# Feed-forward part of an encoder layer: the first product by one level of Strassen's scheme, its result through DRAM, the second product in two token halves

## The chip, the cores and the metric

The kernel runs on one core of a Trainium2 chip. The metric is device time in microseconds. The times of the kernel before are 1242.28, 1242.99 and 1244.46 us (median 1242.99). The traced execution spans 1241.3 us from its first to its last instruction. The engines are PE (matmuls, with PEld for its weight loads), DVE (vector), ACT (scalar), POOL and SP; SP issues the DMAs here.

## The reference

One DeepNorm encoder layer over 784 tokens: 16 meta tokens, 512 of a prompt and 256 of a sample (the last two give the 768 output rows). The model width is 1024, the feed-forward width 4096. The mixer (latent attention beside a bidirectional gated delta rule) is not touched; what follows it is

```
h  = layer_norm(alpha * h + mix, ln1_g, ln1_b)            # [768, 1024] real tokens
ff = square(relu(h @ w_ff1)) @ w_ff2                      # w_ff1 [1024, 4096], w_ff2 [4096, 1024]
h  = layer_norm(alpha * h + ff, ln2_g, ln2_b)             # alpha = 2 ** 0.25
return h[:, N_META:]
```

All of it is fp32. The kernel keeps that accuracy by splitting each operand of a matmul in a high and a low part (`split`: a cast on ACT, line 212, gives the high part, a subtraction on DVE, line 213, the low part) and adding three matmuls, high x high, high x low and low x high.

## The kernel before

The program has four stages: input norm and projections, delta rule, attention, and from about 640 us on the output projection, the first norm and the feed forward. Instructions are written in loops; a planner in the framework then sets each engine's order from its estimates of durations, and tiles of a pool go round in a fixed number of buffers, so that a new tile waits for the last reader of the one whose place it takes. Each engine works strictly in its order; SP issues the DMAs in its own order, and a DMA that waits holds back those behind it.

Tokens are taken in the order `TO` (six tiles of 128, two halves of 384). At the output projection, after three token tiles, `h1_half(0)` (L1065) transposes the normed tokens of one half on PE (L1069), scales them on ACT into `full` (L188) and splits them into `h1h`, `h1l`, features on partitions. After all six come the first matmuls of the feed forward on half 0 (`w1_mm`, L1058) for two weight tiles loaded ahead, then `h1_half(1)`.

The feed forward runs over 8 groups of `NG` = 4 tiles of 128 hidden features. For each tile `w1_load` (L1050) loads 128 columns of w_ff1 (0.52 MB) into the space `LTf` and splits them; `w1_mm` does 2 token halves x 8 feature tiles x 3 = 48 matmuls of 128x384 into a pair of PSUM banks `d` (L1061). ACT takes the relu out of PSUM (L1142), DVE squares (L1143), and the result is split into `fh`, `fl`. 128 rows of w_ff2 (0.52 MB) are loaded (L1150) and split into `w2h`, `w2l`. At the end of a group the second product runs: 6 token tiles x 2 column halves x 4 hidden tiles x 3 = 144 matmuls of 128x512 (L1167); each of the 12 PSUM banks of a group is added to `acc` in SBUF by DVE (L1171; the first group with the factor alpha, L1169). So PE does 1536 matmuls of 128x384 and 1152 of 128x512. The rows `rb2` scale `acc` for the residual (L1158). In the last group each token tile is normed, scaled (L1184 to L1186) and stored.

## Time and profile before

| what | value |
|---|---|
| median of three runs | 1242.99 us |
| profiled execution, span | 1241.3 us (1.7 below the median of the runs) |
| PE busy | 1168.4 us (94%), granted clock 0.973 on average |
| DVE busy | 717.2 us (58%) |
| ACT busy | 511.2 us (41%) |
| DMA moved | 126.49 MB, 102 GB/s on average |

A row of the profile names the line of the kernel, the engine, the operation, and the tiles written and read. Busy time is the sum over a group's instructions, a mean is of one, and matmuls overlap in the pipeline, so that the distance of two starts, not the mean duration of one, is what a matmul costs. The granted clock is a share of 2.4 GHz. A chain of waits follows the work that ended last back through what released each step.

### The profile page before, as it was taken

What the parts mean: (1) busy time and instruction counts of PE and PEld (TensorE: products, weight loads), DVE (VectorE), ACT (ScalarE), POOL (GpSimd) and SP (SyncE); (2) the same over time, 40 slices, a digit from 0 to 9 for tenths busy, and PEclk for the clock granted to TensorE, in tenths of its full rate; (3) what the DMA queues carried; (4) which work ended last, traced back from release to release, by engine and by line L of the source; (5) the groups of instructions that cost most, each with busy time, mean ns of one, the idle gap of its engine ahead of it and who ended that gap; (6) DMA issues with size and microseconds to landing.
All of it is one profiled execution on the core that took longest, in us unless ns stands there. A gap on an engine that the chain in (4) does not pass through costs nothing.

```text
span 1241.3 us, 18703 instructions
## 1 busy us (share of the span) xinstructions
PE 1168.4 (94%) x7468; PEld 1021.7 (82%) x7468; DVE 717.2 (58%) x1136; ACT 511.2 (41%) x974; POOL 171.8 (14%) x201
## 2 busy tenths in 40 slices
PE   5978879998999999989999899999999999999995
PEld 4867879998889877756758798989898989899994
DVE  8567668697967867684456584334243424343348
ACT  5475655324645666563545521203030303121113
POOL 2144554024223221020100000000000000000000
PEclk9888899999999999999999899999999999999998
DMA  5147764522497845340210230303030303131002
GB/s 202 50 111 182 183 166 142 122 92 90 143 268 220 250 132 137 124 140 31 93 52 35 85 102 30 106 24 114 1 119 17 119 18 102 35 100 36 1 1 102
DMA packets 92202, 126.49 MB, mean 102 GB/s; under 512 B 34946, under 2 KB 63362, under 8 KB 92114
## 3 DMA queue, kind: packets, MB, share of 16 engines
q1 hardware_dynamic: 92114, 125.28, 33.9%
q8 instruction: 59, 0.97, 0.3%
q14 instruction: 29, 0.24, 0.1%
HBM read 98.73 MB, written 26.53 MB: 101 GB/s over the span
## 4 chain that ended last, share of the span: by engine, by line
PE 78%; DVE 9%; DMA 5%; ACT 3%; issue 2%; SPq 1%; POOL 1%; DVEq 0%; ACTq 0%; POOLq 0%
PE d L1061 21%; PE b L1167 21%; PE d L331 7%; PE b L1103 5%; DMA x<-gD 3%; PE v L1000 3%; PE c L1003 3%; PE d L969 3%; PE d L704 2%; PE b L837 2%; PE b L853 2%; PE b L877 2%; PE b L870 2%; DVE LP L598 1%; DVE tm L596 1%
## 5 line engine op out<-in xcount | busy, mean ns | idle before, releaser
L1061 PE MATMUL d<-h1h,w1h 128*128 128x384 f32 x512 | 171.5, 337 | 1.3 <-ACT LT L1142 1.3
L1061 PE MATMUL d<-h1l,w1h 128*128 128x384 f32 x512 | 172.0, 336 | 0.0
L1061 PE MATMUL d<-h1h,w1l 128*128 128x384 f32 x512 | 171.9, 336 | 0.0
L1167 PE MATMUL b<-w2l,fh 128*128 128x512 f32 x384 | 151.3, 394 | 0.0
L1167 PE MATMUL b<-w2h,fh 128*128 128x512 f32 x384 | 150.5, 392 | 0.0
L1167 PE MATMUL b<-w2h,fl 128*128 128x512 f32 x384 | 147.6, 389 | 0.0
L1171 DVE TENSOR_TENSOR acc<-acc,b 128x512 f32<-128x512 f32 x84 | 55.9, 685 | 137.9 <-PE b L1167 137.9
L331 PE MATMUL d<-hTh,wl 128*128 128x384 f32 (+1 forms) x352 | 124.7, 354 | 4.2 <-DVE wl L213 4.2
L331 PE MATMUL d<-hTh,wh 128*128 128x384 f32 (+1 forms) x352 | 125.5, 356 | 2.1 <-ACT ks L188 2.1
L212 ACT CAST w2h<-LT 128x1024 fp32r<-128x1024 f32 x32 | 31.9, 1045 | 230.9 <-PE b L1167 212.3
L331 PE MATMUL d<-hTl,wh 128*128 128x384 f32 (+1 forms) x352 | 125.9, 358 | 0.1
L1061 PEld LDWEIGHTS d<-h1h,w1h 128*128 128x128 f32 x512 | 96.3, 189 | 2.7 <-ACT LT L1142 1.6
L1061 PEld LDWEIGHTS d<-h1l,w1h 128*128 128x128 f32 x512 | 96.7, 189 | 0.9 <-DVE h1l L213 0.3
L1061 PEld LDWEIGHTS d<-h1h,w1l 128*128 128x128 f32 x512 | 96.7, 189 | 0.6 <-DVE w1l L213 0.3
L213 DVE TENSOR_TENSOR w1l<-LT,w1h 128x1024 fp32r<-128x1024 f32 x32 | 39.2, 1224 | 88.9 <-ACT w1h L212 88.7
L1167 PEld LDWEIGHTS b<-w2h,fl 128*128 128x128 f32 x384 | 72.1, 188 | 16.1
L1167 PEld LDWEIGHTS b<-w2h,fh 128*128 128x128 f32 x384 | 72.1, 188 | 15.9
L1167 PEld LDWEIGHTS b<-w2l,fh 128*128 128x128 f32 x384 | 72.2, 188 | 13.7
L212 ACT CAST w1h<-LT 128x1024 fp32r<-128x1024 f32 x32 | 33.5, 1050 | 100.3 <-PE d L1061 100.2
L331 PEld LDWEIGHTS d<-hTh,wl 128*128 128x128 f32 x352 | 68.3, 194 | 6.7 <-DVE wl L213 4.6
L331 PEld LDWEIGHTS d<-hTh,wh 128*128 128x128 f32 x352 | 68.1, 193 | 6.7 <-issue 3.4
L331 PEld LDWEIGHTS d<-hTl,wh 128*128 128x128 f32 x352 | 68.1, 193 | 2.9 <-issue 1.5
(316 smaller groups left out, 2265.6 us busy)
## 6 DMA issues: line engine op xcount, KB each, us to landing
LT<-in_w_ff SPq DMA_DIRECT2D x64, 512.0 KB, 3.3
wr<-in_w_in SPq DMA_DIRECT2D x22, 512.0 KB, 3.3
x<-gD SPq DMA_DIRECT2D x16, 560.0 KB, 5.6
KV<-vD SPq DMA_DIRECT2D x26, 256.0 KB, 4.4
U<-UD SPq DMA_DIRECT2D x26, 256.0 KB, 5.2
UD<-ua SPq DMA_DIRECT2D x16, 256.0 KB, 5.1
wor<-in_w_out SPq DMA_DIRECT2D x8, 512.0 KB, 6.5
TB<-tD SPq DMA_DIRECT2D x52, 64.0 KB, 2.5
```

Source lines behind the costliest of these rows:

```text
L212: S.copy(hi, src)
L213: return (eng or V).tensor_sub(lo, src, hi.bitcast(F32))
L331: T.matmul(ps[:, s, :c1 - c0], lhsT=a[:, k, :], rhs=b[:, k, c0:c1], start=(k == 0 and i == 0), stop=(k == KT - 1 and i == 2))
L704: T.matmul(ps[:, s, :HR], lhsT=a[:, k], rhs=b[:, cs], start=(k == 0 and i == 0), stop=(k == 2 and i == 2))
L837: T.matmul(ps[:, j * P:(j + 1) * P], lhsT=TB[:, j], rhs=KV[:, j], start=True, stop=True)
L969: T.matmul(ps[:, :w], lhsT=q[:, qs], rhs=kt[:, k0:k0 + w], start=True, stop=True)
L1000: T.matmul(ps[:, t * P:(t + 1) * P], lhsT=p[:, c0:c0 + P], rhs=dg, start=True, stop=True)
L1003: T.matmul(po[:m, :nq], lhsT=Vs[j][:, t0 + bi, :m], rhs=pt[:, :nq], start=(bi == 0), stop=(bi == ntl - 1))
L1061: T.matmul(ps[:, s, :HR], lhsT=a[:, k, :], rhs=b[:, k, s * HR:(s + 1) * HR], start=(k == 0 and i == 0), stop=(k == KT - 1 and i == 2))
L1103: T.matmul(ps, lhsT=x[:, k, :], rhs=y[:, cs], start=(k == 0 and i == 0), stop=(k == 3 and i == 2))
L1167: T.matmul(ps, lhsT=a[:, qs], rhs=b[:, cs], start=(f == 0 and i == 0), stop=(f == NG - 1 and i == 2))
L1171: V.tensor_add(acc[:, ti, cs], acc[:, ti, cs], ps)
```

## The change

The first product is written as [C11 C12; C21 C22] = A B with A the transposed w_ff1 (its two halves of hidden features by its two halves of input features) and B the normed tokens (two halves of input features by the two token halves). Sixteen rounds `m` take the tiles m and m + 16 of hidden features together. Each has seven products of 12 matmuls 128x384 (L1073 in the changed kernel) on weight blocks or sums of them: with B11, T2, B21, T1, T3, B22 and T4, where the T's are differences of the token quadrants, made once (L1150 to L1163). In a round DVE makes four sums of weight blocks (s12 at L1174 and L1175, then L1186, L1191), ACT and DVE split seven weight operands, and DVE combines the seven PSUM results into four quadrants `fo_` in `LTf` (L1179 to L1195); one is copied by ACT (L1178). ACT does the relu and the square in SBUF (L1198, L1199), and the round's four quadrants (0.79 MB) are stored to the DRAM tile `FD` (L1200). PSUM is cut in two rings, `w` and `b`, of four banks each; weight operands have nine buffers.

The second product follows when all rounds are done, in two token halves. A half keeps its 3 token tiles x 2 column halves in six PSUM banks over all 32 hidden tiles, so `acc` is touched once per bank (12 times in all, L1264). For each half all of w_ff2 is loaded and split (`w2_load`, L1226) and the half's quadrants are read back from `FD` (`f_load`, L1218, 0.39 MB per round). The last `NL` = 4 hidden tiles are kept and run token tile by token tile, after which each is normed and stored as before. The places in `LTf`: rounds alternate between 0..1.5D and 1.5D..3D for `fo_` and between 3D..5D and 5D..7D for the weights; w_ff2 tile n lies in n % 4 * D.

```diff
...
+    fq = {}
+    HQ = 4
+    def w1_raw(m):
+        o = 3 * D + m % 2 * 2 * D
+        wr = LTf[:, o:o + 2 * D].rearrange("p (q k c) -> p q k c", q=4, k=HQ)
+        ld(wr[:, 0:2], I["w_ff1"][m].rearrange("p (q k) c -> p q k c", q=2))
+        ld(wr[:, 2:4], I["w_ff1"][m + 16].rearrange("p (q k) c -> p q k c", q=2))
+        return wr
+    def w1_split(src):
+        wh, wl = (fv.tile([P, HQ, P], F32R, name=n, bufs=9) for n in ("w1h", "w1l"))
+        split(src, wh, wl)
+        return wh, wl
+    def prod(w, n, ps=None):
+        ps = ps if ps is not None else nbank()
+        (wh, wl), (bh, bl) = w, fq[n]
+        for k in range(HQ):
+            for i, (a, b) in enumerate(((wh, bh), (wh, bl), (wl, bh))):
+                T.matmul(ps[:, :HR], lhsT=a[:, k, :], rhs=b[:, k, :],
+                         start=(k == 0 and i == 0), stop=(k == HQ - 1 and i == 2))
+        return ps[:, :HR]
+    nb = [0]
+    def nbank():
+        nb[0] += 1
+        return bank("bw"[nb[0] % 2])
+    RAW0 = 0
+    def h1_full(s, k, full):
+        ps = bank()
+        for i in range(3):
+            T.transpose(ps[:, i * P:(i + 1) * P], acc[:, s * 3 + i, k * P:(k + 1) * P], ident)
+        act(full, ps[:, :HR], AF.Identity, bias=col("l1b", k), scale=col("l1g", k))
+        return full
+    def raw0(k):
+        return LTf[:, RAW0 + k * HR:RAW0 + (k + 1) * HR]
     for half in range(2):
...
         if half == 1:
-            banks_set(b=4, d2=2)
+            banks_set(w=4, b=4)
...
-            h1h = h1p.tile([P, KT, NR], F32R, name="h1h")
-            h1l = h1p.tile([P, KT, NR], F32R, name="h1l")
+            eh = ExitStack()
+            h1p = pool(eh, "h1p", 1, "left")
+            for n in ("B11", "B21"):
+                fq[n] = [h1p.tile([P, HQ, HR], F32R, name=n + x) for x in "hl"]
...
-            ahead = {ft: w1_load(ft) for ft in range(2)}
+            ahead = {}
+            for m in range(2):
+                wr = LTf[:, 6 * D:7 * D].rearrange("p (q k c) -> p q k c", q=2, k=HQ)
+                ld(wr, I["w_ff1"][m].rearrange("p (q k) c -> p q k c", q=2))
+                ahead[m] = [w1_split(wr[:, i]) for i in range(2)]
...
                 if ti == 3:
...
+                    for k in range(KT):
+                        f = h1_full(0, k, raw0(k))
+                        split(f, *(x[:, k % HQ] for x in fq["B11" if k < HQ else "B21"]))
                 if ti == 5:
                     for w in ahead.values():
-                        w1_mm(*w, 0)
-                    h1_half(1)
+                        w[:] = [prod(x, n, bank("w")) for x, n in zip(w, ("B11", "B21"))]
     ex.close()
-    banks_set(b=4, d2=2)
...
+    eq = ExitStack()
+    hq = pool(eq, "hq", 1)
+    for n in ("T2", "T1", "T3", "B22", "T4"):
+        fq[n] = [hq.tile([P, HQ, HR], F32R, name=n + x) for x in "hl"]
+    fu = pool(eq, "fu", 2)
+    for k in range(HQ):
+        b12, b22 = (h1_full(1, k + HQ * i, fu.tile([P, HR], F32, name=n)) for i, n in enumerate(("p5s", "b22")))
+        split(b22, *(x[:, k] for x in fq["B22"]))
+        t1, t2 = (fu.tile([P, HR], F32, name=n) for n in ("u2", "u3"))
+        V.tensor_sub(t1, b12, raw0(k))
+        V.tensor_sub(b12, b22, b12)
+        V.tensor_sub(t2, b22, t1)
+        split(t2, *(x[:, k] for x in fq["T2"]))
+        split(t1, *(x[:, k] for x in fq["T1"]))
+        split(b12, *(x[:, k] for x in fq["T3"]))
+        V.tensor_sub(t2, t2, raw0(k + HQ))
+        split(t2, *(x[:, k] for x in fq["T4"]))
+    FD = dp.tile([16, P, 4, HR], F32, name="FD")
+    for m in range(16):
+        wr = w1_raw(m)
+        p1, p2 = ahead.get(m, (None, None))
+        if p1 is None:
+            p1 = prod(w1_split(wr[:, 0]), "B11")
+        o = m % 2 * 4 * HR
+        fo_ = LTf[:, o:o + 4 * HR].rearrange("p (q c) -> p q c", q=4)
+        sm1 = fv.tile([P, 2, HQ, P], F32, name="s12", bufs=2)
+        V.tensor_add(sm1[:, 0], wr[:, 2], wr[:, 3])
+        V.tensor_sub(sm1[:, 1], sm1[:, 0], wr[:, 0])
+        p6 = prod(w1_split(sm1[:, 1]), "T2")
+        u2 = fu.tile([P, HR], F32, name="u2")
+        S.copy(fo_[:, 0], p1)
+        V.tensor_add(u2, fo_[:, 0], p6)
+        if p2 is None:
+            p2 = prod(w1_split(wr[:, 1]), "B21")
+        V.tensor_add(fo_[:, 0], fo_[:, 0], p2)
+        p5 = prod(w1_split(sm1[:, 0]), "T1")
+        u4 = fu.tile([P, HR], F32, name="p5s")
+        V.tensor_add(u4, u2, p5)
+        V.tensor_sub(wr[:, 2], wr[:, 0], wr[:, 2])
+        p7 = prod(w1_split(wr[:, 2]), "T3")
+        u3 = fu.tile([P, HR], F32, name="u3")
+        V.tensor_add(u3, u2, p7)
+        V.tensor_add(fo_[:, 3], u3, p5)
+        V.tensor_sub(wr[:, 1], wr[:, 1], sm1[:, 1])
+        p3 = prod(w1_split(wr[:, 1]), "B22")
+        V.tensor_add(fo_[:, 1], u4, p3)
+        p4 = prod(w1_split(wr[:, 3]), "T4")
+        V.tensor_sub(fo_[:, 2], u3, p4)
+        for q in ((0, 1), (1, 4)):
+            f = fo_[:, q[0]:q[1]]
+            S.activation(f, f, AF.Relu)
+            S.activation(f, f, AF.Square)
+        st(FD[m], fo_)
+    eq.close()
+    ef.close()
+    eh.close()
+    e7 = ExitStack()
+    fw = pool(e7, "fw", 2)
+    fo = pool(e7, "fo", 1)
...
-    NG = 4
...
-            V.tensor_mul(rl, rl, rl)
...
-                    V.tensor_add(acc[:, ti, cs], acc[:, ti, cs], ps)
...
+    def f_load(s, m):
+        fr = fw.tile([P, 2, HR], F32, name="fr", bufs=2)
+        ld(fr, FD[m, :, s::2, :])
+        fh, fl = (fw.tile([P, 2, HR], F32R, name=n, bufs=3) for n in ("fh", "fl"))
+        split(fr, fh, fl)
+        return fh, fl
+    def w2_load(n, ft):
+        o = n % 4 * D
+        wr = LTf[:, o:o + D]
+        ld(wr, I["w_ff2"][ft * P:(ft + 1) * P, :])
+        wh, wl = (fw.tile([P, D], F32R, name=n, bufs=5) for n in ("w2h", "w2l"))
+        return split(wr, wh, wl), wh, wl
+    NL = 4
+    rb2 = None
+    seq = [(m, i) for m in range(16) for i in range(2)]
+    for s in range(2):
+        po = [[bank(x) for _ in range(2)] for x in (("w", "w", "b"), ("b", "w", "w"))[s]]
+        last = []
+        for n, (m, i) in enumerate(seq):
+            if i == 0:
+                fh, fl = f_load(s, m)
+            x, wh, wl = w2_load(n, m + 16 * i)
+            if s == 0 and n == 2:
+                rb2 = rows2(2)
+                for ti in range(6):
+                    for j, fn in enumerate((V.tensor_mul, V.tensor_add)):
+                        y = fn(acc[:, ti], acc[:, ti], rb2[:, j])
+                        tc.add_manual_dep(y.ins, x.ins.name, NOSYNC, reason="not before it is needed")
+                rb2 = rows2(4)
+            last.append((n, i, fh, fl, wh, wl))
+            if n >= len(seq) - NL and n < len(seq) - 1:
+                continue
+            for g in range(3):
+                for n_, i_, fh_, fl_, wh_, wl_ in last:
+                    qs = slice(g * P, g * P + P)
+                    for h in range(2):
+                        cs = slice(h * 512, h * 512 + 512)
+                        for j, (a, b) in enumerate(((fh_, wh_), (fh_, wl_), (fl_, wh_))):
+                            T.matmul(po[g][h], lhsT=a[:, i_, qs], rhs=b[:, cs], start=(n_ == 0 and j == 0),
+                                     stop=(n_ == len(seq) - 1 and j == 2))
+                if n == len(seq) - 1:
+                    ti = s * 3 + g
+                    t = TO[ti]
+                    a = acc[:, ti]
+                    for h in range(2):
+                        cs = slice(h * 512, h * 512 + 512)
+                        V.scalar_tensor_tensor(a[:, cs], a[:, cs], ALPHA, po[g][h], ALU.mult, ALU.add)
+                    mv = fw.tile([P, 2], F32, name="mv")
+                    dst = O["yp"][t * P:(t + 1) * P, :] if t < 4 else O["ys"][(t - 4) * P:(t - 3) * P, :]
+                    norm_stats(a, P, mv, fw)
+                    for h in range(2):
+                        cs = slice(h * 512, h * 512 + 512)
...
+                        st(dst[:, cs], a[:, cs])
+            last = []
+    e7.close()
...
```

SP's order in the feed forward before (names: `LT` is the space `LTf`; `rb2` the rows of the second norm), from the first groups on:

```order
L1053 DMA LT_525<-in_w_ff1 128x1024 x3
L1128 DMA rb2_7310<-in_rows 128x1024 x2
L1053 DMA LT_525<-in_w_ff1 128x1024
L1150 DMA LT_525<-in_w_ff2 128x1024 x3
L1053 DMA LT_525<-in_w_ff1 128x1024
L1150 DMA LT_525<-in_w_ff2 128x1024
L1053 DMA LT_525<-in_w_ff1 128x1024 x3
L1150 DMA LT_525<-in_w_ff2 128x1024 x4
L1053 DMA LT_525<-in_w_ff1 128x1024 x4
```

And in the changed kernel where the first product ends and the second begins (`FD` written at L1200, read back into `fr` at L1218):

```order
L1200 DMA FD_7014<-LT_525 128x1536 x2
L1226 DMA LT_525<-in_w_ff2 128x1024
L1218 DMA fr_9235<-FD_7014 128x2x384
L1218 DMA fr_9287<-FD_7014 128x2x384
L1213 DMA rb2_9298<-in_rows 128x1024 x2
L1200 DMA FD_7014<-LT_525 128x1536
L1226 DMA LT_525<-in_w_ff2 128x1024
L1218 DMA fr_9357<-FD_7014 128x2x384
L1218 DMA fr_9409<-FD_7014 128x2x384
L1226 DMA LT_525<-in_w_ff2 128x1024 x2
L1218 DMA fr_9461<-FD_7014 128x2x384
L1226 DMA LT_525<-in_w_ff2 128x1024 x5
```

Stores and loads that go through `FD` now stand among the loads of w_ff2, and the last of the stores stands behind two of `fr` and two of `rb2`.

ACT's order in the feed forward before, one stretch of a group with its relu (L1142) and its casts:

```order
L1142 ACTIVATE LT_525<-d2_9914 128x768
L212 CAST fh_9965<-LT_525 128x768
L212 CAST w1h_10105<-LT_525 128x1024
L1142 ACTIVATE LT_525<-d2_9979 128x768
L212 CAST fh_10030<-LT_525 128x768
```

And in the changed kernel at the same boundary, from the last round's relu (L1198) on:

```order
L1198 ACTIVATE LT_525<-LT_525 128x1152
L212 CAST w2h_9242<-LT_525 128x1024
L1199 ACTIVATE LT_525<-LT_525 128x1152
L212 CAST fh_9237<-fr_9235 128x768
L212 CAST fh_9289<-fr_9287 128x768
L212 CAST fh_9359<-fr_9357 128x768
L212 CAST w2h_9265<-LT_525 128x1024
```

The first casts of the second product are now interleaved with the last relu and square.

DVE's order before, where one group's sums to `acc` end and the next tiles' splits stand:

```order
L213 TENSOR_TENSOR w2l_8324<-LT_525,w2h_8323 128x1024
L1171 TENSOR_TENSOR acc_5093<-acc_5093,b_8183 128x512
L213 TENSOR_TENSOR w2l_8389<-LT_525,w2h_8388 128x1024
L213 TENSOR_TENSOR w2l_8454<-LT_525,w2h_8453 128x1024
L213 TENSOR_TENSOR w2l_8687<-LT_525,w2h_8686 128x1024
L213 TENSOR_TENSOR w1l_8329<-LT_525,w1h_8328 128x1024
L1143 TENSOR_TENSOR LT_525<-LT_525 128x768
L213 TENSOR_TENSOR fl_8254<-LT_525,fh_8253 128x768
L213 TENSOR_TENSOR w1l_8394<-LT_525,w1h_8393 128x1024
L1143 TENSOR_TENSOR LT_525<-LT_525 128x768
L213 TENSOR_TENSOR fl_8319<-LT_525,fh_8318 128x768
```

And in the changed kernel in the middle of the first product, from the last split that reads one round's weights (`w1l_8771`) past the sum `s12_8954`, which reads the weights loaded into the same place:

```order
L213 TENSOR_TENSOR w1l_8771<-LT_525,w1h_8770 128x512
L1190 TENSOR_TENSOR LT_525<-u3_8606,w_8573 128x384
L1193 TENSOR_TENSOR LT_525<-p5s_8586,w_8614 128x384
L213 TENSOR_TENSOR w1l_8796<-LT_525,w1h_8795 128x512
L1174 TENSOR_TENSOR s12_8954<-LT_525 128x512
L1195 TENSOR_TENSOR LT_525<-u3_8606,b_8632 128x384
L213 TENSOR_TENSOR w1l_8816<-s12_8812,w1h_8815 128x512
L1175 TENSOR_TENSOR s12_8954<-s12_8954,LT_525 128x512
L1186 TENSOR_TENSOR LT_525<-LT_525 128x512
L213 TENSOR_TENSOR w1l_8836<-LT_525,w1h_8835 128x512
L1191 TENSOR_TENSOR LT_525<-LT_525,s12_8812 128x512
L1179 TENSOR_TENSOR u2_8690<-LT_525,b_8677 128x384
```

The sums to `acc` are gone; in their place stand sums of weights and of PSUM results between the splits, and the sum of newly loaded weights stands four instructions behind the split that frees their place.

## Rows read from the trace of the kernel before

**Rows 1.** Span and mean granted TensorE clock of the core.

```profile
core 0: 1241.3 us, clock 0.973
```

**Rows 2.** The page's chain of waits: shares by engine, then by line.

```profile
PE 78%; DVE 9%; DMA 5%; ACT 3%; issue 2%; SPq 1%; POOL 1%; DVEq 0%; ACTq 0%; POOLq 0%
PE d L1061 21%; PE b L1167 21%; PE d L331 7%; PE b L1103 5%; DMA x<-gD 3%; PE v L1000 3%; PE c L1003 3%; PE d L969 3%; PE d L704 2%; PE b L837 2%; PE b L853 2%; PE b L877 2%; PE b L870 2%; DVE LP L598 1%; DVE tm L596 1%
```

**Rows 3.** Windows: stretch, length, busy us by engine, PEclk, DMA share, rate.

```profile
694.14:731.15 37.01, 31.38 (x170) 30.08 (x169) 26.35 (x33) 18.19 (x28) 0.00 (x0) 0.91 0.30 100
...
694.00:698.00 4.00, 1.18 (x10) 0.91 (x8) 2.68 (x7) 1.63 (x2) 0.00 (x0) 1.00 0.88 288
...
770.95:1195.41 424.46, 424.46 (x2170) 388.74 (x2170) 159.79 (x180) 93.92 (x105) 0.00 (x0) 1.00 0.18 60
...
1222.90:1241.30 18.40, 5.48 (x24) 4.15 (x23) 14.85 (x35) 5.80 (x11) 0.00 (x0) 0.72 0.31 114
```

**Rows 4.** Chain of waits within the feed forward: start us, us, what.

```profile
1071.37 2.76 PE b L1167 x12
...
1076.93 21.98 PE b L1167 x96
...
1098.91 30.18 PE d L1061 x174
...
1137.69 2.76 PE b L1167 x12
```

**Rows 5.** Timeline of PE, start of feed forward: start us, us, what, [idle].

```profile
698.61 1.09 PE L1069 MATMUL b<-cst,acc 128*128 128x128 f32 x4 [3.43 <-ACT acc L1111]
...
700.57 1.54 PE L1069 MATMUL b<-cst,acc 128*128 128x128 f32 x6 [0.88 <-ACT full L188]
...
702.87 0.52 PE L1061 MATMUL d<-h1h,w1l 128*128 128x384 f32 x1
...
703.19 0.52 PE L1061 MATMUL d<-h1h,w1h 128*128 128x384 f32 x1
...
714.04 0.45 PE L1061 MATMUL d<-h1h,w1h 128*128 128x384 f32 x1 [1.32 <-ACT LT L1142]
```

**Rows 6.** Groups from 640 us on: what, count, busy us, mean ns, idle.

```profile
L1171 DVE TENSOR_TENSOR acc<-acc,b 128x512 f32<-128x512 f32 x84 | 55.9, 685 | 137.9 <-PE b L1167 137.9
...
L212 ACT CAST w2h<-LT 128x1024 fp32r<-128x1024 f32 x32 | 31.9, 1045 | 230.9 <-PE b L1167 212.3 <-DMA LT<-in_w_ff 18.2 <-PE b L1103 0.4
...
L212 ACT CAST fh<-LT 128x768 fp32r<-128x768 f32 x32 | 26.7, 836 | 43.6 <-DVE LT L1143 43.6
...
L1158 DVE TENSOR_TENSOR acc<-acc,rb 128x1024 f32<-128x1024 f32 x12 | 13.9, 1217 | 0.0
...
L188 ACT ACTIVATE full<-b,cols 128x384 f32<-128x384 f32 x16 | 9.9, 666 | 1.5 <-DVE h1l L213 0.8 <-PE b L1069 0.7
...
L213 DVE TENSOR_TENSOR h1l<-full,h1h 128x384 fp32r<-128x384 f32 x16 | 8.3, 555 | 7.7 <-ACT h1h L212 7.7
...
L212 ACT CAST h1h<-full 128x384 fp32r<-128x384 f32 x16 | 7.4, 510 | 0.0
...
L1033 DVE TENSOR_TENSOR LT<-LT,v 128x384 f32<-128x384 f32 x8 | 4.2, 550 | 5.1 <-PE v L1032 4.8
...
L213 DVE TENSOR_TENSOR ml<-LT,mh 128x512 fp32r<-128x512 f32 x6 | 4.0, 683 | 1.0 <-ACT mh L212 1.0
...
L212 ACT CAST mh<-LT 128x512 fp32r<-128x512 f32 x6 | 3.6, 614 | 12.9 <-PE b L1103 7.7 <-DVE LT L1033 5.2
```

**Rows 7.** DMA issues: what, queue, count, KB each, median us to landing.

```profile
LT<-in_w_ff SPq DMA_DIRECT2D x64, 512.0 KB, 3.3
...
rb<-in_rows SPq DMA_DIRECT2D x6, 512.0 KB, 5.4
...
tD<-LT SPq DMA_DIRECT2D x6, 512.0 KB, 3.5
```

More of the change, by code (lines that the diff above doesn't have):

```diff
@@ L1064, in h1_half @@
-    def h1_half(s):
-        for k in range(KT):
-            ps = bank()
-            for i in range(3):
-                T.transpose(ps[:, i * P:(i + 1) * P], acc[:, s * 3 + i, k * P:(k + 1) * P], ident)
-            full = os_.tile([P, HR], F32, name="full")
-            cs = slice(s * HR, (s + 1) * HR)
-            act(full, ps[:, :HR], AF.Identity, bias=col("l1b", k), scale=col("l1g", k))
-            split(full, h1h[:, k, cs], h1l[:, k, cs])
+    fq = {}
[6 more added lines that the diff above has]
+        return wr
@@ L1122, in body @@
-    fw = pool(ef, "fw", 2)
-    fs = pool(ef, "fs", 2)
-    fo = pool(ef, "fo", 1)
+    eq = ExitStack()
[15 more added lines that the diff above has]
+        split(t2, *(x[:, k] for x in fq["T4"]))
@@ L1186, in body @@
                         V.tensor_add(a[:, cs], a[:, cs], rb2[:, 1, cs])
-                    st(dst[:, cs], a[:, cs])
-    ef.close()
+                        st(dst[:, cs], a[:, cs])
+            last = []
+    e7.close()
 def kernel(**inputs):
```

65 lines of the change are left out of this document (removed).

## Prediction

> **What bounds the kernel now.** I read the clock and span first [rows 1]: 0.973 of 2.4 GHz, so PE works at its upper level nearly throughout. The chain of waits comes next [rows 2]: PE holds 78% of it, and the two products of the feed forward 21% each; no other line comes near. The windows then show whether PE is the limit there at every moment [rows 3]: from 770.95 to 1195.41 us PE is busy in 424.46 of 424.46 us at clock 1.00, DVE in 160, ACT in 94, DMA has a share of 0.18. So a matmul taken out there is worth its full time, and anything on another engine is worth nothing until PE waits for it. The chain inside a group gives the prices [rows 4]: 174 matmuls of 128x384 in 30.18 us, 0.1734 each; 96 of 128x512 in 21.98 us, 0.229 each. They add up: a group from 1071.37 to 1137.69 is 66.32 us, and 192 x 0.1734 + 144 x 0.229 = 66.3. What the change adds therefore decides at three places: where the first product starts, whether its rounds keep PE fed, and where the second product begins.
>
> All sums go against the profiled span of 1241.3 us; the median of the runs lies 1.7 above it, which I add at the end.
>
> **Matmuls saved: -33.3.** 16 rounds x 7 x 12 = 1344 matmuls of 128x384 instead of 1536: 192 x 0.1734 = 33.3 us. The second product keeps its 1152.
>
> **Start of the first product: +4 (bounds +1 to +9).** Before, PE waits 0.88 and 1.32 us here, beside 3.43 for the normed tokens, which stays [rows 5]. After those waits matmuls start 0.32 apart (702.87, 703.19), the lower clock level, for about a dozen: 12 x (0.32 - 0.173) = 1.8. So 0.88 + 1.32 + 1.8 = 4.0 us were lost already. In the changed kernel 120 matmuls of the first two rounds (168 less the 48 done ahead), 20.8 us of PE, stand against the making of the second half's operands: per quadrant column 4 differences and 5 low parts, 36 DVE operations of 128x384 at 0.555 (the h1l row) behind one `full` of 0.67 [rows 6], so the last is ready 20.7 us after the first transpose. By the order 28 matmuls (4.9 us) stand behind it: 25.6 - 20.8 = 4.8. Two matmul groups (T4 of round 0, B11 of round 2) want PSUM banks which DVE frees late in this queue: +1.6, three operations of 0.55. Nine more weight splits and sums stand on DVE ahead of the norm of the last token tile, three of them not hidden: 3 x 0.68 = 2.0. Less the 4.0: 4.4, taken as 4. If DVE's backlog hides wholly behind the matmuls, only the bank waits remain (+1); if the cold stretch comes back and twice as many splits are exposed, +9.
>
> **The rounds: 0 (bounds 0 to +20).** PE needs 84 x 0.1734 = 14.56 us a round. DVE does 18 operations: 11 of 128x512 from SBUF at 0.683 (ml) and 7 of 128x384 from PSUM at 0.550 (L1033) [rows 6]: 11.4 us. To this comes one wait: the weights of a round go where those of the round before last lay, the split of its T4 operand frees the place, and the sum s12 of the new weights stands four instructions behind it on DVE. The three between cover 2 x 0.55 + 0.68 = 1.8 of it. A load of 0.52 MB takes 3.3 us where moving it at the 288 GB/s seen at most takes 1.8, so 1.5 goes otherwise [rows 3, 7]; with the round's other half (1.05 MB together) beside it, 3.6 + 1.5 = 5.1. The wait is 1.5 to 3.3; with its middle DVE is at 11.4 + 2.4 = 13.8, below PE's 14.56, with its end at 14.7, where the weight buffers' lead still covers 14 rounds. ACT is at 7 x 0.614 for casts, 0.51 for the copy, 2 x 0.51 and 2 x some 1.2 for relu and square (768 elements take 0.836, 1024 take 1.045, so 1152 some 1.2) = 8.2. The square on ACT has no row; between 0.84 and 2 us for the large one ACT stays under 11. The evictions that go (84 x 0.685 and 12 alike on DVE) lie beside PE: nothing gained. Upper bound: DVE 1.5 us above PE in 14 rounds.
>
> **From the first product to the second: +16 (bounds +10 to +20).** Count from the end of the last T4 matmul. DVE's last combination takes 0.6; the read of `fr` waits for it, since `fr` lies in the place of a round's buffer, and lands 3.3 to 4 later. ACT has in its order relu (1.2), cast of w_ff2 (1.05), square (1.2), cast of `fr` (0.84): the first matmul comes at 5. It finds one weight tile: 18 matmuls, 4.1 us, to 9.1. The next weight tile goes into a place that the last `FD` store still reads. That store waits for the square (4.2) and stands on SP behind two reads of `fr` (0.79 MB) and two loads of `rb2` (1.05 MB): these need 6.4 at 288 GB/s, to 7.0, its own 0.79 MB 2.7 more. With the 1.5 that goes otherwise, the store has landed at 11.3. Meanwhile w_ff2 tile 4 and two more reads of `fr` (1.31 MB) were issued ahead; they move until 14.4. Then the awaited tile, 1.8 + 1.5, to 17.7, and its cast, 1.05: the second group of matmuls starts at 18.7 instead of 4.1. That is 14.6 of loss, and 1.8 for the lower clock after such idling, as at the start: 16.4, taken as 16. Lower bound: every transfer in its own time by its nearest row, the store 1.5 x 3.5 from 4.2 to 9.4 [rows 7], the load 3.3 and the cast 1.05 to 13.8, less 4.1, 9.7. Upper bound: store and load each held up as the `rb` loads are (5.4 against 3.3), 2 x 2.1 more, 20.
>
> The Trainium skill speaks to this place ("DMA: Bandwidth & Descriptors", section "Anatomy of one DMA — SWDGE (gpsimd) path"): a transfer costs about 2.0 us fixed plus its bytes at 436 GB/s. By that estimate the store takes 3.8 and the load 3.2 (the row has 3.3), the group starts at 12.3 and the loss is 8.2. The rows show no rate above 288 GB/s, with 3.3 for one load alone and 5.4 for loads side by side; the page's fit is for another path than SP's queue.
>
> **The second product: 0.** A weight tile gives PE 18 x 0.229 = 4.1 us. Per two tiles (8.24 us) DMA brings 1.05 MB of w_ff2 and 0.39 MB of `fr`, 175 GB/s against the 288 seen; DVE has 2 x 1.22 (as L1158) + 0.95, ACT 2 x 1.045 + 0.836. Twelve operations of L1158's kind (14 us) are spread over slack. The second half starts in fresh banks with its loads ahead.
>
> **The end: -1 (bounds -2 to +1).** Before, the last window has PE busy for 5.48 of 18.40 us [rows 3], so matmuls end near 1228.4 and 12.9 us of eviction, norm and stores follow for two token tiles that DVE does together. After, the earlier tile is done under the 24 matmuls of the last: about 12.
>
> Sum: -33.3 + 4 + 0 + 16 + 0 - 1 = -14.3, a span of 1227.0; with the 1.7 of the median 1228.7, predicted as 1229. Own range 1219 to 1238, from the bounds of start and boundary.
>
> **Rivals.**
>
> *The boundary is cheap.* The reads, `rb2` and the store move side by side without holding each other up: its loss is 9.7 as in the lower bound, 6 less: 1223. For it: the DMA share is 0.18 in the feed forward, so nothing else is moving. Against it: at 694 to 698 the share is 0.88 at 288 GB/s, and the bytes ahead of the awaited tile are 4.5 MB. The Trainium skill's rule above would give 1221.
>
> *DVE becomes the bound of the rounds.* Place: the wait of s12 on its load. If the two weight loads move behind the `FD` store of a round (1.84 MB for all, 6.4 + 1.5 = 7.9 us), the wait is 6.1 and a round takes 17.5: 14 x 2.94 = 41, less what the nine weight buffers hold ahead, about four products x 2.08 = 8: +33, so 1262, slower than before. It decides from DVE rounds of 15.1 on (over 8 us in 14 rounds), and the kernel is slower than before from 16.2 (14 x 1.6 - 8 = 14.4), a wait of 4.8. For it: at most 0.8 us of slack in a sum of 18 prices. Against it: successive DVE operations overlap a little, and the store is issued half a round away from the loads.
>
> *The second product is short of data.* If the loads of w_ff2 and `fr` followed each other (3.9 + 2 x 3.3 = 10.5 us per two tiles against 8.24): 32 x 2.3 = 72, 1301. Against it: window rows with 0.88 DMA share show transfers running side by side, and 175 GB/s is well below that.
>
> *The matmuls saved come back as waits.* Start +9, boundary +20 and a few us in the rounds: about 1243, no change.
>
> **Chances.** Forecast 0.60, cheap boundary 0.13, DVE-bound rounds 0.14 (0.05 of it short of break-even, between 1231 and 1248), no change 0.07, short of data 0.05, something unforeseen 0.01. A measurement of this kernel can tell about 0.2% (2.5 us) from no change. Faster is the forecast, the cheap boundary and a part of the milder DVE case: 0.75; within 0.2% 0.07; slower 0.18 (the rest of the DVE case, the shortage, and the forecast with all its bounds on the bad side). The range goes from 1216 (the cheap boundary with a start at its lower bound, 1220, and a little for prices that overlap) to 1248 (the middle of the DVE case); outside lie the shortage, the full DVE case and a better end still, some 0.17.
>
> **What would show it.** Matmuls of the first product 1344 at starts 0.173 apart, and rounds of 14.6 us with PE busy throughout: right; DVE busy near 100% with PE idle "behind w1l" or a sum: the DVE case. At the boundary two gaps of PE, about 5 and 9.6 us, the second ended by a load of w_ff2: right; a second gap of 5 or less: the cheap boundary. In the second product PE gaps ended by DMA: the shortage. At the start a loss against before of 1 to 9 us on waits for DVE. Wrong altogether if the gaps sum to more than 33 us.

## The result, and the profile after

The changed kernel takes 1224.36 us (median of 4 runs, 1223.05 to 1226.39) against 1242.63 for the kernel before: ratio 0.9857, 95% interval 0.9839 to 0.9875, 18 us faster. 1229 was predicted, in a range of 1216 to 1248. The profiled execution spans 20.0 us less than that of before [rows 1]:

```profile
core 0: 1221.3 us, clock 0.973
```

The windows of the new profile (columns as in [rows 3]) show the stages one after the other: the start of the feed forward, the rounds, the boundary between the products, the second product, the end:

```profile
690.47:731.00 40.53, 32.96 (x179) 30.88 (x179) 36.87 (x80) 29.85 (x56) 0.00 (x0) 0.92 0.17 55
770.95:920.00 149.05, 149.05 (x859) 149.05 (x858) 103.83 (x178) 77.84 (x121) 0.00 (x0) 1.00 0.33 117
929.00:975.00 46.00, 33.34 (x128) 26.64 (x127) 30.65 (x29) 18.26 (x19) 0.00 (x0) 0.85 0.64 208
975.00:1060.00 85.00, 85.00 (x376) 70.39 (x376) 36.86 (x33) 29.56 (x31) 0.00 (x0) 1.00 0.62 209
1060.00:1195.00 135.00, 135.00 (x597) 111.78 (x597) 70.09 (x87) 51.02 (x60) 0.00 (x0) 1.00 0.50 166
1203.00:1221.30 18.30, 5.44 (x24) 4.16 (x23) 12.88 (x30) 3.81 (x8) 0.00 (x0) 0.77 0.23 86
```

In the rounds and in the second product PE is busy in every microsecond at clock 1.00, as it was [rows 3]. DVE has 104 of 149 us in the rounds. The two places where PE loses time are the first and the third window.

The prices of a matmul are read from the chain of waits (start, length, what, count), as in [rows 4]:

```profile
737.83 2.08 PE w L1073 x12
...
767.03 2.08 PE w L1073 x12
...
975.88 2.72 PE w L1256 x12
```

From 737.83 to 767.03 two rounds of 84 matmuls pass: 29.20 / 168 = 0.1738 each, so a round is 14.6 us. In the second product 12 take 2.72, that is 0.2267 each; before it was 0.2290 [rows 4]. That difference, times 1152, is 2.6 us.

The start of the feed forward on PE (idle before in brackets), answering to [rows 5]:

```profile
666.25 1.81 PE L1089 MATMUL b<-cst,acc 128*128 128x128 f32 x12
...
695.34 5.19 PE L1089 MATMUL b<-cst,acc 128*128 128x128 f32 x20 [4.27 <-ACT acc L1137]
...
701.82 0.45 PE L1073 MATMUL w<-T2h,w1h 128*128 128x384 f32 x1 [1.29 <-ACT T2h L212]
...
716.72 0.45 PE L1073 MATMUL w<-T4h,w1h 128*128 128x384 f32 x1 [1.34 <-DVE u L1179]
```

PE waits 4.27 for the normed tokens, 1.29 for the first operand and 1.34 for a PSUM bank (a further wait of 0.54 for an operand is not shown): 7.4 us where before it was 3.43 + 0.88 + 1.32 = 5.6. That the last of them is for a bank is read from DVE's row, which ends where the matmul starts and which reads a product of T2 out of PSUM; the first parts of T4 had been cast long before:

```profile
716.12 0.54 DVE L1179 TENSOR_TENSOR u<-LT,w 128x384 f32<-128x384 f32 x1
```

The first of PE's rows also says where this stage begins. In the kernel before the same transposes stand here:

```profile
670.57 1.82 PE L1069 MATMUL b<-cst,acc 128*128 128x128 f32 x12
```

They begin 4.3 us earlier now, ahead of everything that the prediction priced.

The boundary on PE: the last matmul of the first product, the first of the second, and the first on the second weight tile:

```profile
929.38 0.34 PE L1073 MATMUL b<-T4h,w1l 128*128 128x384 f32 x1
...
934.91 0.79 PE L1256 MATMUL w<-w2h,fh 128*128 128x512 f32 x1 [5.20 <-ACT fh L212]
...
949.02 2.07 PE L1256 MATMUL w<-w2h,fh 128*128 128x512 f32 x4 [7.46 <-ACT w2h L212]
```

Two gaps, 5.20 and 7.46 us. ACT's rows there:

```profile
930.34 1.16 ACT L1198 ACTIVATE LT<-LT 128x1152 f32<-128x1152 f32 x1 [7.24 <-DVE LT L1195]
...
932.34 1.16 ACT L1199 ACTIVATE LT<-LT 128x1152 f32<-128x1152 f32 x1
...
934.03 0.83 ACT L212 CAST fh<-fr 128x768 fp32r<-128x768 f32 x1 [0.52 <-DMA fr<-FD]
...
947.93 4.12 ACT L212 CAST w2h<-LT 128x1024 fp32r<-128x1024 f32 x4 [2.23 <-DMA LT<-in_w_ff]
```

Relu (1.16), a cast, the square (1.16), then the cast of `fr` at 934.03, behind which the first matmul starts. And SP's issues (start of issue, what):

```profile
930.37 1.22 SPq L1218 DMA_DIRECT2D fr<-FD  x2
931.64 1.06 SPq L1213 DMA_DIRECT2D rb<-in_rows  x2
933.53 0.33 SPq L1200 DMA_DIRECT2D FD<-LT  x1
933.96 0.73 SPq L1226 DMA_DIRECT2D LT<-in_w_ff  x1
935.88 3.24 SPq L1218 DMA_DIRECT2D fr<-FD  x2
942.63 0.81 SPq L1226 DMA_DIRECT2D LT<-in_w_ff  x2
```

The store of `FD` is issued at 933.53, behind two reads of `fr` and two loads of `rb2`. The chain of waits says how long PE's second gap hangs on it and on the load behind it:

```profile
933.53 9.09 DMA FD<-LT
942.63 5.19 DMA LT<-in_w_ff
```

The store takes 9.09 us, the load of the tile into its place 5.19; the cast follows at 947.93. Elsewhere the same transfers take less (columns as in [rows 7]; the medians rest on few transfers, since the trace holds the landing of 15 of the 98 loads and of one of the 16 stores):

```profile
LT<-in_w_ff SPq DMA_DIRECT2D x98, 512.0 KB, 4.2
FD<-LT SPq DMA_DIRECT2D x16, 768.0 KB, 3.3
```

Two windows of the same profile tell what DMA moves meanwhile, in the middle of this burst and over the whole of it:

```profile
938.00:942.00 4.00, 3.56 (x12) 2.46 (x10) 0.57 (x1) 0.00 (x0) 0.00 (x0) 0.78 1.01 410
930.40:945.80 15.40, 6.65 (x18) 4.94 (x18) 3.22 (x4) 5.60 (x6) 0.00 (x0) 0.78 0.82 291
```

From 938 to 942 the DMA engines are busy throughout (share 1.01) at 410 GB/s.

### The profile page after: what moved, and what is told of

It reads as the page before. It is cut to its first block, busy times and chain, and to the rows that moved or that the text cites. A ratio compares the mean times of both kernels' runs of the same rounds, so it can differ in the third digit from the quotient of the medians.

```text
span 1221.3 us, 19070 instructions
## 1 busy us (share of the span) xinstructions
PE 1133.6 (93%) x7276; PEld 987.9 (81%) x7276; DVE 813.7 (67%) x1336; ACT 614.8 (50%) x1146; POOL 171.0 (14%) x201
## 4 chain that ended last, share of the span: by engine, by line
PE 73%; DVE 11%; DMA 7%; ACT 4%; issue 2%; SPq 1%; POOL 1%; DVEq 0%; ACTq 0%; POOLq 0%
PE w L1256 14%; PE w L1073 9%; PE b L1073 9%; PE d L331 7%; PE b L1256 7%; PE b L1129 4%; DMA x<-gD 3%; PE v L1000 3%; PE c L1003 3%; PE d L969 3%; PE d L704 2%; PE b L837 2%; PE b L853 2%; PE b L877 2%; PE b L870 2%
## 5 line engine op out<-in xcount | busy, mean ns | idle before, releaser
L213 DVE TENSOR_TENSOR w2l<-LT,w2h 128x1024 fp32r<-128x1024 f32 x64 | 78.0, 1223 | 57.8 <-ACT w2h L212 57.8
L1256 PE MATMUL w<-w2h,fh 128*128 128x512 f32 x256 | 99.0, 398 | 12.7 <-ACT w2h L212 7.5
L1256 PE MATMUL w<-w2l,fh 128*128 128x512 f32 x256 | 101.0, 395 | 0.0
L1256 PE MATMUL w<-w2h,fl 128*128 128x512 f32 x256 | 99.6, 391 | 0.0
L212 ACT CAST w1h<-LT 128x512 fp32r<-128x512 f32 x80 | 48.8, 616 | 49.3 <-PE w L1073 20.7
L1256 PEld LDWEIGHTS w<-w2h,fh 128*128 128x128 f32 x256 | 49.0, 192 | 23.6 <-ACT w2h L212 7.9
L213 DVE TENSOR_TENSOR w1l<-LT,w1h 128x512 fp32r<-128x512 f32 x80 | 54.6, 687 | 6.6 <-ACT w1h L212 6.4
L1256 PEld LDWEIGHTS w<-w2l,fh 128*128 128x128 f32 x256 | 49.1, 192 | 10.2
L1198 ACT ACTIVATE LT<-LT 128x384 f32<-128x384 f32 (+1 forms) x32 | 27.1, 847 | 48.9 <-DVE LT L1195 33.4
L1256 PE MATMUL b<-w2l,fh 128*128 128x512 f32 x128 | 50.1, 391 | 0.0
L1256 PE MATMUL b<-w2h,fh 128*128 128x512 f32 x128 | 49.9, 396 | 0.0
```

Source lines behind the costliest of these rows:

```text
L212: S.copy(hi, src)
L213: return (eng or V).tensor_sub(lo, src, hi.bitcast(F32))
L1198: S.activation(f, f, AF.Relu)
L1256: T.matmul(po[g][h], lhsT=a[:, i_, qs], rhs=b[:, cs], start=(n_ == 0 and j == 0), stop=(n_ == len(seq) - 1 and j == 2))
```

## The experiments

Times of the experiments are compared with runs of the kernel before on the same chip, whose median lay between 1242.0 and 1243.6; where two experiments ran on different chips, their ratios to it are the fairer comparison.

**The scheme taken out: eight products instead of seven (e4_eight).** `prod2` is `prod` over two operand pairs in one PSUM bank.

```diff
-        p6 = prod(w1_split(sm1[:, 1]), "T2")
...
-        V.tensor_sub(fo_[:, 2], u3, p4)
+        for q, (x, y) in enumerate((("B11", "B21"), ("T1", "B22"), ("B11", "B21"), ("T1", "B22"))):
+            a = ws[q // 2 * 2:q // 2 * 2 + 2]
+            ps = done.pop(m) if q == 0 and m in done else prod2(a, (x, y))
+            S.activation(fo_[:, q], ps, AF.Relu)
+            V.tensor_mul(fo_[:, q], fo_[:, q], fo_[:, q])
```

> The changed kernel with eight products per round instead of seven (plain quadrants, two products added up in one PSUM bank, no sums on DVE, relu out of PSUM on ACT, square on DVE): the same staging through FD and the same second product, without Strassen's scheme. Theory (the scheme is worth its 192 matmuls at 0.1734, and costs only the making of operands at the start): 33.3 us more for the matmuls, less about 3 for the waits at the start: 1254. So FD and the halves alone cost about 11 to 12 against the kernel before. Rival (DVE's and ACT's load of the scheme slows PE in the rounds): eight products cost clearly less than 30 us more, 1250 or below.

Measured: 1239.4 us (ratio to before 0.9968, 0.9953 to 0.9984). The expectation failed by 15 us: without the scheme the kernel is only 15 us slower than with it, and 3.4 us faster than the kernel before. The rival's time (1250 or below) came true, but not its reason: it looked in the rounds, where PE waits in neither kernel, and the theory had put 3 us on the start. The list of PE's waits (engine, line, waited for: us, times, longest) has the reason; one more wait of 0.4 is all that it leaves out from the first transposes on:

```profile
PE w L1236 <- ACT w2h L212: 5.4, 1, 5.4
PE w L1236 <- ACT fh L212: 2.2, 1, 2.2
PE b L1100 <- ACT p5s L188: 0.4, 1, 0.4
```

The waits of the start (7.4) are gone, and the boundary has 7.6 instead of 12.7. From the first transposes to the last matmul of the first product this kernel takes 286.5 us with 1536 matmuls, the changed one 263.1 with 1344: 23.4 more, not 33.3. So the scheme gives 33.3 and takes back 9.9 at the start and, by the same count over the second product, 6.5 at the boundary. The 9.9 stand complete after the first two rounds: the 168th matmul of the changed kernel starts 9.9 us later after the first transpose than the 168th here. The 6.5 are not the scheme's alone, since this kernel also takes the relu out of PSUM and squares on DVE, so that ACT has less to do ahead of the first cast. The remaining 1.7 lies ahead of the feed forward.

**The two loads of `rb2` later (e2_rb_late).**

```diff
-            if s == 0 and n == 2:
-                rb2 = rows2(2)
+            if s == 0 and n == 6:
+                rb2 = rows2(2, x)
...
+            if x is not None:
+                tc.add_manual_dep(y.ins, x.ins.name, NOSYNC, reason="not before it is needed")
```

> The changed kernel with the two loads of rb2 (1.05 MB) issued eight w_ff2 tiles later, so that the last FD store is no longer behind them on SP. Theory (the store is slow because 1.84 MB were issued ahead of it and share the rate): the store lands up to 1.05 MB / 288 GB/s = 3.6 us earlier, the second gap falls from 7.5 to about 4, the time to about 1221. Rival (the store's own latency and the square before it set the gap): gap 7 or more, time unchanged at 1224.

Measured: 1220.74 us, and the second gap on PE:

```profile
945.92 1.69 PE L1258 MATMUL w<-w2h,fh 128*128 128x512 f32 x4 [3.86 <-ACT w2h L212]
```

3.86 instead of 7.46, 3.6 us less, which is what 1.05 MB take at 288 GB/s. The match is in part chance. By the chain of waits the store now takes 4.13 us, 5.0 less, and the load behind it 5.84, 0.65 more; the awaited tile lands 4.3 us earlier, and the first tile's matmuls end 0.7 earlier. What the number does show is that the store is late because of what was issued ahead of it.

**The awaited tile in another place (e1_slots).**

```diff
-        o = n % 4 * D
+        o = (n + 3) % 7 * D
```

> The changed kernel with the loaded w_ff2 tiles in a ring of seven places of LT that begins behind the last round's FD source (3D, 4D, 5D, 6D, 0, D, 2D), so that the second tile no longer waits for the last FD store. Theory (the second gap of PE at the boundary is the wait for that store and then for the load into its place): the second gap of 7.5 us is gone; the first grows from 5.2 to about 8.5, since five casts of w_ff2 tiles now stand on ACT ahead of the last square and the cast of the first f; with the lower clock after it about 11 of loss instead of 17.4, so about 6 us less, 1218. Rival (the gap is the rate of all the transfers put off to the boundary, whatever place they go to): a gap of 5 us or more stays behind the first or second tile, and the time stays within 2 us of 1224.

Measured: 1226.63 us, no gain: 2 us above the changed kernel, by ratios (0.9871, 0.9844 to 0.9898, against 0.9857) not clear of noise. The first gap grew to 8.35 as expected and the wait for the store is gone, but a new gap stands in the middle of the first weight tile:

```profile
952.22 2.08 PE L1256 MATMUL w<-w2h,fl 128*128 128x512 f32 x4 [7.47 <-DVE fl L213]
```

It ends with `fl`, the low part of the first operand. DVE's rows say what stood ahead of it:

```profile
940.99 6.90 DVE L1244 TENSOR_TENSOR acc<-acc,rb 128x1024 f32<-128x1024 f32 x6 [2.67 <-DMA rb<-in_rows]
...
951.22 0.95 DVE L213 TENSOR_TENSOR fl<-fr,fh 128x768 fp32r<-128x768 f32 x1
```

The residual scaling (L1244, 1.15 us each) had waited behind the late weight tiles before; with the tiles early, it comes between DVE and the operand that PE waits for. The rival had said that a gap of 5 us or more would stay, and one did, but not for its reason, the rate of the transfers. Neither the theory nor the rival named DVE's queue, to which the wait moved.

**Both (`rb2` late as in e2, another ring of places), and the first `fr` read early (e3_boundary).**

```diff
-        o = n % 4 * D
+        o = (n + 4) % 7 * D
...
-        fr = fw.tile([P, 2, HR], F32, name="fr", bufs=2)
+        if s == 0 and m == 0:
+            fr = LTf[:, 3 * D:3 * D + 2 * HR].rearrange("p (a c) -> p a c", a=2)
+        else:
+            fr = fw.tile([P, 2, HR], F32, name="fr", bufs=2)
...
+                rb2 = rows2(2, x)
```

> The changed kernel with w_ff2 tiles in seven places from 4D on, rb2 later, and the first f read into the weight place of round 14 in LT, which is free during round 15. Theory: PE waits at the boundary only for DVE's last combination, ACT's relu and two casts, about 3.7 us, and loses about 2 to the lower clock: 5.7 instead of 17.4, so 11.7 us less, 1212 to 1213. Rival (transfers at the boundary are short of rate anyway): the loss only moves behind later w_ff2 tiles, time 1218 or more.

Measured: 1213.48 us, ratio to before 0.9759 (0.9732 to 0.9786), 11 us less than the changed kernel and the fastest version here. PE's waits in the second product are these two:

```profile
933.23 2.07 PE L1261 MATMUL w<-w2h,fh 128*128 128x512 f32 x4 [3.51 <-ACT w2h L212]
...
954.02 1.20 PE L1261 MATMUL w<-w2h,fh 128*128 128x512 f32 x4 [1.60 <-ACT w2h L212]
```

5.1 us of gaps instead of 12.7. The last store is no faster here: it stands behind four w_ff2 tiles in place of the `rb2` loads and takes 9.51 us by the chain of waits. So it is not the `rb2` loads as such that make a store late, but what moves ahead of it, and what the boundary cost was the order of its transfers and the place of two tiles: PE now meets that store only at the fifth tile (the gap of 1.60).

**Slack of the rounds: the square on DVE (e5_square_dve), one sum nine times (e8_nine_sums).**

```diff
-            S.activation(f, f, AF.Square)
+            V.tensor_mul(f, f, f)
```

> The changed kernel with the square of each round on DVE (128x384 and 128x1152) instead of ACT. Theory (the rounds have slack on DVE: 11 operations start 0.60 apart and 7 start 0.47 apart, 9.9 us, and the wait of the weight sum for its load is 1.7 us a round, 27.3 us in 16): 0.47 + 1.4 more make 13.5 of 14.56, PE waits for nothing in the rounds, time 1224 within 2. Rival (DVE is at its limit as counted with full durations, 11.4 + 1.7 + 1.9 = 15.0): rounds of 15.0, 6 us more less the lead of the buffers, and PE idle behind DVE in the rounds.

Measured: 1227.9 us (1225.9 to 1229.4). Every one of the last 14 rounds still takes 14.60 us and PE waits for nothing in them, so the rounds have room for 1.9 us of DVE more. The time is 1.9 us above the expected band. The second gap at the boundary is 9.0 in this profile; why it grew is not shown.

```diff
-        V.tensor_sub(sm1[:, 1], sm1[:, 0], wr[:, 0])
+        for _ in range(9):
+            V.tensor_sub(sm1[:, 1], sm1[:, 0], wr[:, 0])
```

> The changed kernel with the second weight sum of each round (L1175) done nine times over instead of once: 8 x 0.60 = 4.8 us more of DVE a round, nothing else changed. Theory (DVE has 14.56 - 11.6 = 2.9 us of slack a round, then it is the bound): rounds of 9.9 + 1.7 + 4.8 = 16.4, 1.8 over PE in 14 rounds, 26, less up to 8 that the weight buffers hold ahead: 18 to 26 us more, about 1245. Rival (the wait for the load disappears under the added work): rounds of 14.7, at most 2 us more, 1226.

Measured: 1248.81 us, slower than the kernel before (ratio 1.0035, 1.0017 to 1.0052): the predicted rival, brought about. From the first transposes to the end of the first product it is 287.5 us instead of 263.1, 24.3 more. That is inside the theory's 18 to 26, but not as the theory made it up: by the starts of the matmuls 15 of them lie in the last 14 rounds (between 14.6 and 19.4 us each, 15.7 in the mean, where 16.4 was expected), less than its lower end, and 9 at the start, where it had none and where two rounds put 2 x 4.8 us more on DVE. In the middle of the rounds DVE is at its limit:

```profile
770.00:900.00 130.00, 125.47 (x705) 122.96 (x704) 125.39 (x220) 63.27 (x104) 0.00 (x0) 0.99 0.34 120
```

DVE is busy for 96% of this stretch (70% in the rounds of the changed kernel, 104 of 149 us), and PE for 125 of 130 us at 0.99.

**The start: the norm first (e7_norm_first), POOL (e9, e10).** `late` orders an instruction of rounds 0 and 1 behind the last norm; the split of the T4 weights and the sum at L1186 are treated alike.

```diff
-        V.tensor_add(sm1[:, 0], wr[:, 2], wr[:, 3])
+        late(m, V.tensor_add(sm1[:, 0], wr[:, 2], wr[:, 3]))
...
-        p4 = prod(w1_split(wr[:, 3]), "T4")
+        p4 = prod(w1_split(wr[:, 3], m), "T4")
```

> The changed kernel with the sums and splits of weights of the first two rounds kept in DVE's order behind the norm of the last token tile. Theory (the wait of 4.3 us for the normed tokens comes from nine weight operations between the parts of that norm on DVE): the wait falls to under 1 us; the nine operations then stand among the 36 that make the second half's operands, and PE waits about 2 more there: 1222, 1.5 to 2.5 less. Rival (the norm's own chain over DVE and ACT makes the wait): it stays above 3.5 and the time at 1224.

Measured: 1225.36 us. The wait for the normed tokens is gone; the list of PE's waits has these instead, and the stage is 264.9 us against 263.1:

```profile
PE w L1075 <- ACT T2h L212: 2.4, 1, 2.4
...
PE w L1075 <- DVE u L1186: 2.1, 1, 2.1
...
PE b L1091 <- ACT p5s L188: 1.6, 1, 1.6
...
PE b L1091 <- ACT b L188: 1.1, 2, 0.5
```

So the 4.3 us were not to be had from the order. That wherever the weight operations stand, PE waits for the sum of DVE's work fits this, and it fits the start of e8, where 9.6 us more on DVE cost 9.

Two kernels then took work off DVE. e9 is e3_boundary with the order of e7 and eight low parts on POOL; e10 is e3_boundary with twelve on POOL (its third edit, of T4, is like the two shown):

```diff
-        split(b22, *(x[:, k] for x in fq["B22"]))
+        split(b22, *(x[:, k] for x in fq["B22"]), eng=G)
...
-        split(b12, *(x[:, k] for x in fq["T3"]))
+        split(b12, *(x[:, k] for x in fq["T3"]), eng=G)
```

> The kernel of e3_boundary with the order of e7_norm_first and the low parts of B22 and T3 (8 of the 36 operand operations of the start) made by POOL instead of DVE. Theory (the start is bound by the sum of DVE's work there, which is why the norm put first gained nothing by itself): 8 x 0.47 = 3.8 us off DVE are 3 to 4 us off the start, 1210 against 1213.5 for e3_boundary. Rival (the start hangs on the chain norm, transpose, operand, not on DVE's sum; or POOL at 1.08 us an operation is later than DVE): no change, 1213 or more.

> The kernel of e3_boundary with the low parts of B22, T3 and T4 (12 operations) made by POOL, the order of the norm left as it is. Theory: the wait for the normed tokens (4.2) stays, the waits behind it (1.3, 0.5, 0.4) go, so 2 us less, 1211 to 1212. Rival (POOL's 12 x 1.08 = 13 us make T4 late): PE waits for T4's low part, 1214 or more.

Measured: 1221.18 and 1218.25 us, 7.7 and 4.8 slower than e3_boundary (ratios 0.9834 and 0.9817 against 0.9759); from the first transposes to the end of the first product it is 8.5 and 4.5 us more. DVE's rows in e10, at the start:

```profile
702.60 0.55 DVE L1156 TENSOR_TENSOR u<-p5s,LT 128x384 f32<-128x384 f32 x1
...
704.45 1.35 DVE L1158 TENSOR_TENSOR u<-b,u 128x384 f32<-128x384 f32 x1
...
708.26 0.54 DVE L213 TENSOR_TENSOR T1l<-u,T1h 128x384 fp32r<-128x384 f32 x1
```

POOL's in the same microseconds:

```profile
704.38 1.01 POOL L213 TENSOR_TENSOR T3l<-p5s,T3h 128x384 fp32r<-128x384 f32 x1 [0.26 <-POOL B22l L213]
...
705.35 1.31 POOL L213 TENSOR_TENSOR B22l<-b,B22h 128x384 fp32r<-128x384 f32 x1
...
706.62 1.31 POOL L213 TENSOR_TENSOR T3l<-p5s,T3h 128x384 fp32r<-128x384 f32 x1
```

While POOL works, a DVE operation of 128x384 takes 1.35 us instead of 0.55 (the last row, begun in a pause of POOL, has 0.54), and POOL's own takes 1.01 to 1.31. In e9 it is POOL that is held up. Two of its operations, merged in this row, take 5.84 us while DVE, until 703.5, does eight operations at 0.56 (128x384) to 0.70 us:

```profile
699.46 5.84 POOL L213 TENSOR_TENSOR B22l<-b,B22h 128x384 fp32r<-128x384 f32 x2 [80.78 <-ACT B22h L212]
```

So work that was moved came back as waiting, now on one engine and now on the other. The Trainium skill states this ("SBUF — State Buffer", section "SBUF: two separate sides"): a DVE operation with two SBUF inputs and a POOL operation that reads SBUF lock each other out of a shared pair of ports for a whole instruction. The rows of e10 and e9 agree; I had left it out of the expectation. Since the two engines hold each other up, neither run tells what taking work off DVE alone would give.

**The distance of the 128x512 matmuls (e6_before_runs3): the kernel before, with its second product changing banks every three matmuls.**

```diff
-                ps = bank()
-                for f, (fh, fl_, w2h, w2l) in enumerate(ffs):
+            pss = [bank(), bank()]
+            for f, (fh, fl_, w2h, w2l) in enumerate(ffs):
+                for s in range(2):
...
+                        T.matmul(pss[s], lhsT=a[:, qs], rhs=b[:, s * 512:s * 512 + 512],
+                                 start=(f == 0 and i == 0), stop=(f == NG - 1 and i == 2))
```

> The kernel before with its second product written as three matmuls into one PSUM bank, three into the bank of the other column half, and so on, instead of twelve in a row into one bank. In the trace of the changed kernel, which changes banks every three matmuls and evicts only 12 times, 128x512 matmuls start 0.2267 apart, in that of the kernel before 0.2290. Theory (the order of banks makes the difference): they start 0.2267 apart here too and the time falls by 1152 x 0.0023 = 2.6 us, to 1240. Rival (the 96 evictions and new accumulations make it): the distance stays at 0.229 and the time at 1242.8.

Measured: 1243.05 us (ratio 1.0002), and in the chain of waits:

```profile
1076.40 21.98 PE b L1166 x96
```

21.98 for 96, as before. The order of banks is not the cause. Nor do the evictions show: in the kernel before, the three matmuls of a hidden tile follow one another at 226, 229.5 and 232 ns, over and over, with nothing longer where a bank changes, while in the changed kernel, from 975 to 1195 us, every distance is 225 to 228. The distance goes with the operand that is read; whether its place makes it was not tried, and the 2.6 us stay unexplained.

## Why the prediction was right, step by step

| term | predicted | measured, by the profiled spans |
|---|---|---|
| before the feed forward | no term | -4.3 |
| matmuls saved | -33.3 | -33.3 (192, at 0.1734 to 0.1738) |
| start of the first product | +4 | +2.9 (waits +1.8; the rest is what the other rows leave) |
| the rounds | 0 | 0 (14 rounds of 14.60) |
| the boundary | +16 | +17.4 (gaps 12.7, lower clock 4.7) |
| the second product | 0 | -2.6 (0.2267 instead of 0.2290) |
| the end | -1 | 0 (12.9 us after the last matmul, as before) |
| sum | -14.3 | -20 |

The terms that the prediction priced come to -13.0 as measured, against -14.3 predicted: a time of about 1230. That this is so near 1229 is in part luck, since the misses of the single terms cancel. The two terms that it did not price, -2.6 ahead of the feed forward (without 1.7 of scatter, see below) and -2.6 in the second product, bring the sum to -18.2, and the medians differ by 18.3. So by its time alone the result (1224) stands nearer to the rival of the cheap boundary (1223) than to the forecast. The gaps decide between the two: 17.4 us were lost at the boundary, where the forecast has 16 and the rival 9.7.

The boundary was read nearly to the step. Counted from the end of the last T4 matmul (929.55, one distance after its start), the first matmul of the second product comes at 5.4 (predicted 5) and the second weight tile at 19.5 (18.7). The store was predicted to land at 11.3 and landed at 13.1, the load behind it at 17.7 and landed at 18.3. The 288 GB/s of the sums were taken as the most that moves; they are close to the mean of the burst (291), but in its middle DMA moves 410, so 288 is no limit. (The 4.5 MB that the prediction names ahead of the awaited tile include that tile; 3.9 stand ahead.) The clock was under-priced: 1.8 stood for one stretch at its lower level, and there were two, since PE idles twice. The first weight tile's 18 matmuls take 6.65 us instead of 4.08, and the second stretch costs 2.1. e2 confirms that the store hangs on what is ahead of it, and the cheap boundary is refuted, as is the shortage of data (PE has no gap from 975 to 1195 us while DMA moves up to 209 GB/s). The store took 9.09 beside three other kinds of transfers; the one of the 16 stores whose landing is recorded, in the rounds, took 3.3. By the Trainium skill's fit for one transfer ("DMA: Bandwidth & Descriptors", section "Anatomy of one DMA — SWDGE (gpsimd) path") the store is estimated at 3.8 us, near the recorded one and far from the last; the fit is for GpSimd's path, not for SP's queue.

The rounds came out with more room than the sum had. It used mean durations, 0.683 and 0.550, where operations in a row start 0.60 and 0.47 apart, so DVE is busy for 10.5 us of a round (126.0 us in the twelve rounds from 737.83 to 913.03) and not 11.4; the wait for the loads is 1.7 in the mean, at the low end of 1.5 to 3.3:

```profile
L1174 DVE TENSOR_TENSOR s<-LT 128x512 f32<-128x512 f32 x16 | 11.0, 690 | 27.3 <-DMA LT<-in_w_ff 27.3
```

(27.3 us idle in 16 rounds, ended by the load.) The rival of DVE-bound rounds was real as a mechanism, as e8 shows, but it was some 2.4 us a round away: 1.9 more (e5) cost the rounds nothing, 4.8 more (e8) made DVE the limit.

Two terms were missing, and both helped. Of the 4.3 us ahead of the feed forward, 1.1 are there at 320 us, up to where the two programs have the same order on PE, and 1.7 at 350 us. This is taken as scatter of single executions: over the twelve profiles the last matmul of line 837 starts between 512.1 and 516.8. The other 2.6 go with the planner's order: from the start of the delta rule's last matmul of line 837 to the transposes it is 155.2 us in the kernel before and 152.4 to 152.9 in the changed one and all experiments on it except e9 (154.3); e6, with the kernel before's order, has 155.5. Before, PE waits for a sum on DVE in this stretch,

```profile
554.67 0.50 PE L1103 MATMUL b<-woh,mh 128*128 128x512 f32 x1 [3.25 <-DVE acc L1105]
```

and the granted clock is at its lower level from 555.3 to 558.7 behind it (0.89 in the mean from 545 to 560). The new order does not have this wait; it has a longer one elsewhere, so that PE's waits in the stretch sum to 6.9 us before and 6.0 after, and its clock stays at the upper level there. That the order makes the difference is inferred from these twelve profiles, not tried by itself. A change in the feed forward had reordered the attention stage, and the comparison of the two orders would have shown that there was something to price.

The start came out in size, but not in its parts. Against the kernel before it costs 2.9, since that kernel lost 4.0 there too, as the prediction counted, with its first w_ff2 splits in the way of the norm. Of the prediction's parts the bank wait was right (1.6 predicted, 1.34 measured). The sums and splits ahead of the norm cost 0.84 more than before instead of 2.0, and the wait of 4.8 for the last operand did not come: PE waits 1.29 and 0.54 for the first ones. What made up for it is the lower clock behind the first of these waits, which stood only in the upper bound: the 20 transposes from 695.34 take 5.19 us, where 12 take 1.81 at 666.25. Against a kernel with the same staging and plain products, which has none of this (e4), the start costs 9.9: 7.0 are waits, and the rest goes with the clock (0.92 granted in the first window, 1.00 in e4 from 690 to 731).

What e4's expectation made of it, that FD and the halves cost some 12 us by themselves, does not hold: with them and without the scheme the kernel is 3.4 faster than before. But they don't save it in the feed forward. e4's first transposes start at 664.52, 6 us earlier than those of the kernel before, and from there to the end e4 takes 572.0 us and the kernel before 570.7.
